# Block products summed in PSUM from a copy of the first one, and the pooled groups taken in the order 4, 16, 8, 2

## The chip, the cores and the metric

The kernel runs on one core of a Trainium2 chip. A core has engines that work beside each other, each through its own instructions in order: PE (matmuls into PSUM), DVE (elementwise work), ACT (activations, copies, casts), POOL (elementwise work, slower here) and SP, which issues DMA transfers. PSUM is the small memory that PE writes to and that DVE and ACT can read and write; SBUF is the large one. The metric is the device time of one execution in microseconds (us). The program is built by a scheduler that simulates the engines and puts each engine's instructions in an order of its own; priorities and "issue after" marks in the source steer it, and the order in the source is not the order on the chip.

## The reference

Two layers act on a stream of 1024 tokens by 1024 channels (and 256 context tokens, which only the first layer uses). The even layer adds a gated convolution branch and a gated recurrence branch. The odd layer, where most of this change lies, is a pooling mixer:

```
z = h @ w_in                       # 1024 -> 4096: u (2048), g (2048)
for group, w in enumerate((2, 4, 8, 16)):      # 512 channels of u each
    d[group] = mean of u over [t - w/2, t + w/2) in its row of 64 tokens - u
y = concat(d[group] @ w_grp[group]) * scale
x = x + gate * ((y * silu(g)) @ w_out)         # 2048 -> 1024
return rmsnorm(x, final_g)
```

`h` is the normalised stream, scaled and shifted by a conditioning vector. Everything is in float32.

## The kernel before, in words

**Numbers.** A float32 product is made of three products of a faster matmul type: a source is split in a high part (a cast on ACT, L94) and a low part (source minus high part, on DVE or POOL, L95), and high x high, high x low and low x high are accumulated in PSUM (`prod`, L595: 12 matmuls of 128 x 512 for a block of 512 input channels).

**Blocks.** Large projections go through `quad` (L610). It computes two tiles of 128 output channels over all 1024 tokens as a 2 x 2 block product in seven products instead of eight (Strassen's scheme in Winograd's form). The output block (i, h) is channel tile m + i, token half h. On the side of the activations the operands are sums of blocks (`block_sums`, L557: t1 to t4 beside b11, b21, b22, listed in `BOPS`, L51); on the side of the weights `wquad` (L567) loads two tiles of 128 x 1024, makes three sums and a difference on DVE (L583, L584, L585, L590) and splits all seven operands: 1 and 6 on DVE, 2, 5, 7, 4 and 3 on POOL. Then

- product 1 goes into the PSUM tile a, ACT copies it to SBUF as s1 (L616); product 6 goes into b, DVE writes s2 = b + s1 (L621); product 2 is accumulated on a, which is block (0,0);
- product 5 goes into c, ACT copies it to s3 (L629); product 7 is accumulated on b, DVE writes s1 = b + s1 (L636); block (1,1) is s3 + s1, added on POOL, since both are in SBUF;
- product 4 goes into a fourth tile d; block (1,0) is s1 - d, on DVE; product 3 is accumulated on c, and block (0,1) is s2 + c, on DVE.

`put` is what the caller does with a block. PSUM has four banks for such tiles (`psum`, L86). Evacuations have a raised priority (`EVAC`).

**Order of the work.** Up to 763 us: conditioning, norm, the even layer's projections and recurrence, and its gates. 763 to 848: the out-projection of its convolution branch, `woa` (L830), four quads, with each result added to a partial residual in memory (`added`, L802: load, gated add, store). 848 to 905: the norm, and folding of `w_in` with `w_grp`. 905 to 1254: the pooling mixer's input, eight pairs of quads (the loop at L1002, m = 0, 2, ..., 14): a quad of u, whose blocks go to padded tiles (`to_tokens`, L1011), then pooling on DVE (`pool`, L913: log2(w) shifted adds at L928, corrections at the row ends at L937 and L941, the difference at L946, for each of four tiles), and a quad of g with SiLU (`to_gate`, L1018). The product of the two (L1057) and its block sums go to memory (`y_keep`, `y_sums`). In the second to fifth pair two conditioning tiles for the second layer's gate are also computed on DVE (L205). 1254 to 1438: the out-projection in two halves of its input: part 0 in four quads (L1071, blocks added to the residual), part 1 in two quads (L1101) and two halves of a quad without products 5 and 3 (`last_half0`, L1182), whose remaining products come at the end in column pieces, between the steps of the final norm. 1438 to 1462: the last of the norm and the stores.

## Time and profile before

| what | value |
|---|---|
| median of three runs | 1466.99 us (1466.47 to 1467.98) |
| the profiled execution's own time | 1463.63 us |
| its span | 1461.8 us |
| mean granted clock of PE | 0.961 |
| PE busy | 1323.3 us (91%) |
| DVE busy | 1265.6 us (87%) |
| ACT busy | 639.2 us (44%) |
| POOL busy | 739.9 us (51%) |

A busy PE isn't PE at its best pace: matmuls overlap, and at a low granted clock each takes longer. So a stretch is best compared with the number of its matmuls times the distance of two of them at full pace. The idle time printed with a group of instructions is that of its engine just ahead of them, and the name behind it is what ended it. The prediction below shows the rows that it uses.

### The profile page before, as it was taken

How to read it: one execution, taken by the hardware profiler on the slowest of the kernel's cores; microseconds unless marked ns; L12 is line 12 of the kernel's file. 1: busy time of each engine (PE TensorE's matmuls, PEld its weight loads, DVE VectorE, ACT ScalarE, POOL GpSimd, SP SyncE). 2: the span in 40 equal slices, each digit the busy share in tenths (PEclk: the TensorE clock that was granted, in tenths of full speed). 3: DMA queues.
4: the chain of work that ended last, by engine and by line, in shares of the span. 5: the costliest groups of instructions: out<-in, count | busy, mean ns of one | idle time of the engine just before them, and what ended most of it. 6: DMA issues, size and time to landing. Idle time of an engine off the chain costs nothing. (4 is left out here: it accounts for less than half of the span.)

```text
span 1461.8 us, 15892 instructions
## 1 busy us (share of the span) xinstructions
PE 1323.3 (91%) x5664; PEld 1060.8 (73%) x5664; DVE 1265.6 (87%) x1445; ACT 639.2 (44%) x906; POOL 739.9 (51%) x398
## 2 busy tenths in 40 slices
PE   7799989897999889999998989999998997798896
PEld 4478767776777677888886877778777775577675
DVE  7985889798879899997878859999999999986985
ACT  6443584466457624226334345433332223433542
POOL 5273654664557456425327446555435536445642
PEclk9999999999999999999999999999999999899998
DMA  9741212121211223443542475133342135457723
GB/s 362 251 116 39 63 37 73 65 65 34 75 51 52 71 94 119 133 146 120 190 137 98 158 219 169 56 129 129 116 137 86 66 116 173 151 187 241 244 91 115
DMA packets 82867, 181.80 MB, mean 124 GB/s; under 512 B 7778, under 2 KB 27618, under 8 KB 82788
## 3 DMA queue, kind: packets, MB, share of 16 engines
q1 hardware_dynamic: 74340, 176.60, 36.7%
q10 hardware_dynamic: 8448, 4.20, 1.0%
q8 instruction: 44, 0.72, 0.2%
q14 instruction: 35, 0.29, 0.1%
HBM read 136.72 MB, written 44.04 MB: 124 GB/s over the span
## 5 line engine op out<-in xcount | busy, mean ns | idle before, releaser
L681 DVE SCALAR_TENSOR_TENSOR conv<-u,sm,conv 128x1009 f32<-128x1009 f32 (+14 forms) x240 | 300.8, 1272 | 21.9 <-ACT conv L674 18.7
L95 POOL TENSOR_TENSOR wl_wu<-wr_wu,wh_wu 128x1024 fp32r<-128x1024 f32 x16 | 38.7, 2422 | 68.4 <-ACT wh_wu L94 68.4
L95 POOL TENSOR_TENSOR wq_wo<-wr_wo,wq_wo 128x512 fp32r<-128x512 f32 x32 | 49.7, 1558 | 43.8 <-ACT wq_wo L94 42.5
L95 POOL TENSOR_TENSOR wq_g<-wr_g,wq_g 128x512 fp32r<-128x512 f32 x32 | 55.0, 1735 | 31.6 <-ACT wq_g L94 31.6
L94 ACT CAST wq_v<-wr_v 128x512 fp32r<-128x512 f32 x48 | 28.2, 619 | 91.3 <-DVE wr_v L585 45.5
L520 PE MATMUL g<-uh,wh_gw 128*128 128x512 f32 (+1 forms) x96 | 40.1, 419 | 25.7 <-ACT g L523 16.3
L95 POOL TENSOR_TENSOR wq_v<-wr_v,wq_v 128x512 fp32r<-128x512 f32 x32 | 55.3, 1744 | 14.8 <-ACT wq_v L94 11.1
L94 ACT CAST wq_g<-wr_g 128x512 fp32r<-128x512 f32 x48 | 28.2, 619 | 78.7 <-DVE wr_g L585 28.4
L523 ACT ACTIVATE g<-g,sm 128x512 f32<-128x512 f32 (+1 forms) x96 | 53.4, 623 | 18.0 <-PE g L522 10.1
L242 PE MATMUL fold<-gh,wh_wu 128*128 128x512 f32 x128 | 53.6, 420 | 6.3 <-ACT wh_wu L94 6.3
L439 POOL TENSOR_TENSOR g<-g,uc 128x1280 f32<-128x1280 f32 x16 | 47.4, 2963 | 19.9 <-ACT g L523 19.9
L124 PE MATMUL gb<-h0h,wh_gb 128*128 128x512 f32 x128 | 51.7, 404 | 5.5 <-ACT sb L662 5.5
L243 PE MATMUL fold<-gl,wh_wu 128*128 128x512 f32 x128 | 52.8, 413 | 3.7 <-DVE gl L95 3.7
L444 POOL TENSOR_TENSOR g<-g,g 128x1280 f32<-128x1280 f32 x16 | 50.6, 3176 | 9.6 <-ACT g L443 9.6
L457 POOL TENSOR_TENSOR g<-g,g 128x1024 f32<-128x1024 f32 x8 | 19.1, 2387 | 70.6 <-DVE g L454 70.6
L445 DVE SCALAR_TENSOR_TENSOR g<-a,g 128x1280 f32<-128x1280 f32 x16 | 37.1, 2316 | 20.3 <-POOL g L444 20.3
L244 PE MATMUL fold<-gh,wl_wu 128*128 128x512 f32 x128 | 51.7, 413 | 2.7 <-POOL wl_wu L95 2.7
L126 PE MATMUL va<-h0h,wl_va 128*128 128x512 f32 x128 | 49.6, 391 | 3.1 <-POOL wl_va L95 3.1
L125 PE MATMUL gb<-h0l,wh_gb 128*128 128x512 f32 x128 | 51.4, 401 | 0.0
L126 PE MATMUL gb<-h0h,wl_gb 128*128 128x512 f32 x128 | 50.9, 399 | 0.0
L125 PE MATMUL wob<-ybl,wh_wob 128*128 128x512 f32 x128 | 50.3, 394 | 0.0
L126 PE MATMUL ga<-h0h,wl_ga 128*128 128x512 f32 x128 | 50.2, 392 | 0.0
(577 smaller groups left out, 4802.4 us busy)
## 6 DMA issues: line engine op xcount, KB each, us to landing
mod<-modT SPq DMA_DIRECT2D x28, 512.0 KB, 3.9
wr_wu<-wu SPq DMA_DIRECT2D x16, 512.0 KB, 4.1
x_part<-xp SPq DMA_DIRECT2D x32, 256.0 KB, 3.2
xp<-x_part SPq DMA_DIRECT2D x32, 256.0 KB, 4.1
mod<-modT SPq DMA_DIRECT2D x32, 256.0 KB, 3.5
wr_v<-wfold SPq DMA_DIRECT2D x16, 512.0 KB, 3.5
wr_g<-wg SPq DMA_DIRECT2D x16, 512.0 KB, 4.4
yr_t<-y_t SPq DMA_DIRECT2D x16, 512.0 KB, 5.8
```

The lines of the kernel that those rows point to most:

```text
L94: return (nc.scalar.copy(hi, src), eng.tensor_tensor(out=lo, in0=src, in1=hi.bitcast(F32), op=sub))
L95: eng.tensor_tensor(out=lo, in0=src, in1=hi.bitcast(F32), op=sub))
L124: nc.tensor.matmul(ps, hi[:, kc], xh[k][:, cols], start=(k == 0), stop=False)
L125: nc.tensor.matmul(ps, hi[:, kc], xl[k][:, cols], start=False, stop=False)
L126: nc.tensor.matmul(ps, lo[:, kc], xh[k][:, cols], start=False, stop=(k == ks - 1))
L242: nc.tensor.matmul(ps, wh[:, kc], gh[i], start=(i == 0), stop=False)
L243: nc.tensor.matmul(ps, wh[:, kc], gl[i], start=False, stop=False)
L244: nc.tensor.matmul(ps, wl[:, kc], gh[i], start=False, stop=(i == 3))
L439: nc.gpsimd.tensor_tensor(out=ius[d], in0=ius[d], in1=uc, op=mult)
L444: nc.gpsimd.tensor_tensor(out=iu, in0=iu, in1=r, op=mult)
L523: nc.scalar.activation(t[:, a : a + n], ps[:, :n], AF.Sigmoid, bias=col(ob + d * KT + j))
L681: nc.vector.scalar_tensor_tensor(out=acp[:, a:b], in0=us[j][:, a + o : b + o], scalar=col(O_CONVW + 31 * j + k), in1=acp[:, a:b], op0=mult ...
```

## The change

**Products.** `quad` now uses three PSUM tiles. ACT copies product 1 from a into b, inside PSUM. Product 5 goes into c; its part for block (1,1) is handed on at once. Product 6 is accumulated on b, on top of the copy, and the part for block (0,1) is handed on; product 2 on a gives block (0,0). Product 7 on b completes block (1,1) with the kept part, product 3 on c completes block (0,1), and product 4 on b is block (1,0), which needs no add (the sign of t4 is turned for that). A part is kept by an ACT copy to SBUF (`keep_part`) or, where the block is added to a residual that lies in SBUF, added there by the gated DVE add, so that the second part is a second gated add. No add is left on POOL; `quad`'s additions on DVE (L621, L636) are gone. `last_half0` follows the same scheme, with product 4 in a tile of its own, second in order.

**Pooling order.** The host permutes the four groups of channels, in `w_in`, `w_grp`, `scale` and `w_out`, so that the loop meets the widths 4, 16, 8, 2 instead of 2, 4, 8, 16 (two pairs of quads each).

**Order of operands and loads.** `BOPS` and the splitting of the operands follow the new order of products. `wquad` splits operand 5 first on POOL, and 4 last; with `late` (the last weights) 4 before and 5 later. `woa` loads the partial residual straight into the tiles that it is added in. The weights of the next quad of part 0 wait for the last store of y, and the later operands of part 0 for the last SiLU.

```diff
-WINDOWS = (2, 4, 8, 16)
+GROUPS = (1, 3, 2, 0)
+WINDOWS = tuple(2 << g for g in GROUPS)
...
-BOPS = ("b11", "t2", "b21", "t1", "t3", "t4", "b22")
+BOPS = ("b11", "t1", "t2", "b21", "t3", "b22", "t4")
...
         p1 = op(a11, 1, nc.vector)
+        if late:
+            p4 = op(a22, 4, nc.gpsimd)
         s3 = ttile(f"ws_{name}")
         nc.vector.tensor_tensor(out=s3, in0=a11, in1=a21, op=sub)
         nc.vector.tensor_tensor(out=a21, in0=a21, in1=a22, op=add)
         nc.vector.tensor_tensor(out=a11, in0=a21, in1=a11, op=sub)
+        if not late:
+            p5 = op(a21, 5, nc.gpsimd)
         p6 = op(a11, 6, nc.vector)
         p2 = op(a12, 2, nc.gpsimd)
-        p5 = op(a21, 5, nc.gpsimd)
         p7 = op(s3, 7, nc.gpsimd)
         nc.vector.tensor_tensor(out=a12, in0=a12, in1=a11, op=sub)
-        p4 = op(a22, 4, nc.gpsimd)
+        if late:
+            p5 = op(a21, 5, nc.gpsimd)
         p3 = op(a12, 3, nc.gpsimd)
+        if not late:
+            p4 = op(a22, 4, nc.gpsimd)
...
-        a = psum(f"qa_{name}")
+        a, c, b = psum(f"qa_{name}"), psum(f"qc_{name}"), psum(f"qb_{name}")
         prod(a, p1, ops["b11"], True, False)
-        s1 = ttile(f"s1_{name}")
         with tc.high_priority(offset=EVAC):
-            evac_a = nc.scalar.copy(s1, a)
-        b = psum(f"qb_{name}")
-        prod(b, p6, ops["t2"], True, False)
-        s2 = ttile(f"s2_{name}")
+            evac = nc.scalar.copy(b, a)
+        prod(c, p5, ops["t1"], True, False)
         with tc.high_priority(offset=EVAC):
-            evac_v = nc.vector.tensor_tensor(out=s2, in0=b, in1=s1, op=add)
+            put(1, 1, c, 0)
+        prod(b, p6, ops["t2"], False, False)
+        with tc.high_priority(offset=EVAC):
+            put(0, 1, b, 0)
         prod(a, p2, ops["b21"], False, True)
         with tc.high_priority(offset=EVAC):
-            put(0, 0, a, None, None)
-        c = psum(f"qc_{name}")
-        prod(c, p5, ops["t1"], True, False)
-        s3 = ttile(f"s3_{name}")
-        with tc.high_priority(offset=EVAC):
-            nc.scalar.copy(s3, c)
+            put(0, 0, a, None)
...
-        prod(b, p7, ops["t3"], False, True)
+        prod(b, p7, ops["t3"], False, False)
         with tc.high_priority(offset=EVAC):
-            nc.vector.tensor_tensor(out=s1, in0=b, in1=s1, op=add)
-        with tc.high_priority(offset=EVAC):
-            put(1, 1, s3, s1, add)
-        d = psum(f"qd_{name}")
-        prod(d, p4, ops["t4"], True, True)
-        with tc.high_priority(offset=EVAC):
-            put(1, 0, s1, d, sub)
+            put(1, 1, b, 1)
         prod(c, p3, ops["b22"], False, True)
         with tc.high_priority(offset=EVAC):
-            put(0, 1, s2, c, add)
+            put(0, 1, c, 1)
+        prod(b, p4, ops["t4"], False, True)
+        with tc.high_priority(offset=EVAC):
+            put(1, 0, b, None)
         return w
+
+    def keep_part(parts, name, i, x):
+        parts[i] = ttile(f"s{i}_{name}")
+        nc.scalar.copy(parts[i], x)
...
     def woa(m, w, ahead):
-        def put(i, h, x, y, op):
-            if (i, h) == (0, 0):
-                for q in range(2):
-                    x1[m + q] = xtile(f"x1_{m + q}")
-            v = x1[m + i][:, HALF[h]]
-            added(m0, m, i, h, x, y, op, v)
-            square_acc(nacc[h][:, :H], v, (m, i) == (0, h), f"n1q{m}_{i}_{h}")
+        for q in range(2):
+            x1[m + q] = xtile(f"x1_{m + q}")
+
+        def put(i, h, x, part):
+            v, dr = x1[m + i][:, HALF[h]], x1_part[m + i][:, HALF[h]]
+            if part != 1:
+                nc.sync.dma_start(v, dr)
+            nc.vector.scalar_tensor_tensor(out=v, in0=x, scalar=m0[:, 0, 2 * KT + m + i : 2 * KT + m + i + 1],
+                                           in1=v, op0=mult, op1=add)
+            if part != 0:
+                nc.sync.dma_start(dr, v)
+                square_acc(nacc[h][:, :H], v, (m, i) == (0, h), f"n1q{m}_{i}_{h}")
         return quad(w, f"woa{m}", ya, put, ahead)
...
+        def to_tokens(i, h, x, part):
+            if part is None:
                 nc.scalar.copy(token[i][h], rows(x))
+            elif part == 0:
+                keep_part(parts, f"v{m}", i, x)
             else:
-                eng = nc.gpsimd if (i, h) == (1, 1) else nc.vector
-                eng.tensor_tensor(out=token[i][h], in0=rows(x), in1=rows(y), op=op)
-
-        def to_gate(i, h, x, y, op):
+                nc.vector.tensor_tensor(out=token[i][h], in0=rows(x), in1=rows(parts[i]), op=add)
+
+        def to_gate(i, h, x, part):
             v = ys[m + i][:, HALF[h]]
-            if y is None:
-                nc.scalar.activation(v, x, AF.Silu)
-            else:
-                eng = nc.gpsimd if (i, h) == (1, 1) else nc.vector
-                eng.tensor_tensor(out=v, in0=x, in1=y, op=op)
-                nc.scalar.activation(v, v, AF.Silu)
+            if part == 0:
+                keep_part(parts, f"g{m}", i, x)
+                return
+            if part == 1:
+                nc.vector.tensor_tensor(out=v, in0=x, in1=parts[i], op=add)
+                x = v
+            silu[0] = nc.scalar.activation(v, x, AF.Silu)
...
+    def gated(k, v, x):
+        return nc.vector.scalar_tensor_tensor(out=v, in0=x, scalar=m1[:, 0, 2 * KT + k : 2 * KT + k + 1],
+                                              in1=v, op0=mult, op1=add)
+
     for m in range(0, KT, 2):
-        def put(i, h, x, y, op):
-            added(m1, m, i, h, x, y, op)
+        parts = {}
+
+        def put(i, h, x, part):
+            if part == 0:
+                keep_part(parts, f"wo0_{m}", i, x)
+                return
+            t = vtile(f"xp{m}_{i}_{h}")
+            nc.sync.dma_start(t, x1_part[m + i][:, HALF[h]])
+            if part == 1:
+
+                s = x if i == 0 else parts[i]
+                nc.vector.tensor_tensor(out=s, in0=x, in1=parts[i], op=add)
+                x = s
+            gated(m + i, t, x)
+            nc.sync.dma_start(x1_part[m + i][:, HALF[h]], t)
...
     def last_half0(m, w, ahead=None):
         p1, p2, p3, p4, p5, p6, p7 = w
-        a = psum(f"qa_l{m}")
+        a, d, b = psum(f"qa_l{m}"), psum(f"qd_l{m}"), psum(f"qb_l{m}")
+        (x0, x1_), (y0, y1) = [[x1[m + i][:, h] for h in HALF] for i in range(2)]
         prod(a, p1, ops["b11"], True, False)
...
+            evac = nc.scalar.copy(b, a)
+        mm = prod(d, p4, ops["t4"], True, True)
         with tc.high_priority(offset=EVAC):
-            evac_v = nc.vector.tensor_tensor(out=s2, in0=b, in1=s1, op=add)
+            gated(m + 1, y0, d)
...
+            prod(b, p6, ops["t2"], False, False)
         with tc.high_priority(offset=EVAC):
-            gated(m, x1[m][:, HALF[0]], a)
+            gated(m, x1_, b)
+        mm = prod(a, p2, ops["b21"], False, True)
+        with tc.high_priority(offset=EVAC):
+            gated(m, x0, a)
             fin_add(HALF[0], square(m, HALF[0]))
-        mm = prod(b, p7, ops["t3"], False, True)
+        with tc.issue_after(mm.ins):
+            mm = prod(b, p7, ops["t3"], False, True)
         with tc.high_priority(offset=EVAC):
...
+            gated(m + 1, y0, b)
             fin_add(HALF[0], square(m + 1, HALF[0]))
-            vec = gated(m + 1, x1[m + 1][:, HALF[1]], s1)
+            vec = gated(m + 1, y1, b)
```

84 lines of the change are left out of this document (30 added, 54 removed).

## The prediction, made before the changed kernel had run

> **What bounds the kernel now.** I read, in this order, the table of busy time by stretch, the waits of PE, the groups of DVE and POOL, and the timeline at single stalls. First the stretches (length; then busy time and instruction count of PE, weight loads, DVE, ACT, POOL; then granted clock, DMA share, GB/s), those that the change reaches; the third to fifth row are the pairs of quads in which the pooling mixer's input is computed: first pair, six middle pairs, last pair; then the out-projections.
>
> ```profile
> 675.30:763.20 87.90, 87.90 (x387) 72.43 (x386) 69.35 (x143) 36.56 (x50) 28.60 (x14) 1.00 0.47 153
> 763.20:848.00 84.80, 78.11 (x326) 61.21 (x324) 69.98 (x70) 35.49 (x61) 49.26 (x31) 0.98 0.41 130
> ...
> 905.40:1254.30 348.90, 317.64 (x1345) 256.03 (x1344) 326.73 (x418) 117.91 (x207) 172.27 (x111) 0.98 0.35 114
> ```
> ```profile
> 905.58:953.00 47.42, 41.89 (x169) 33.02 (x168) 44.58 (x52) 25.77 (x44) 26.65 (x26) 0.93 0.26 84
> 953.00:1202.58 249.58, 234.74 (x1009) 190.76 (x1008) 232.62 (x314) 73.28 (x133) 117.70 (x71) 0.99 0.34 110
> 1202.58:1254.57 51.99, 41.10 (x170) 32.31 (x168) 49.62 (x54) 18.96 (x30) 27.73 (x15) 0.97 0.49 159
> 1254.57:1437.90 183.33, 161.66 (x664) 128.91 (x662) 149.57 (x151) 75.53 (x117) 97.43 (x56) 0.93 0.51 174
> ```
>
> The pace of PE alone comes from the first matmuls of two products that follow each other (start, duration):
>
> ```profile
> 971.89 0.39 PE L599 MATMUL qc_v<-x_b22h,wq_v 128*128 128x512 f32 x1
> ...
> 974.62 0.39 PE L599 MATMUL qa_g<-x_b11h,wq_g 128*128 128x512 f32 x1
> ```
>
> Twelve matmuls take 2.73 us, 0.2275 each; a quad (84) is 19.1, a pair 38.2. The eight pairs would take 305.8 at this pace and take 348.9: 43.1 over. The out-projections after them hold 672 matmuls' worth (six quads, two last halves of 60, 24 of 512 columns and 48 of 256), 152.9, and take 183.3: 30.4 over. Before 905 only the first out-projection (336 matmuls, 76.4; 84.8 taken) is touched; the stretch ahead of it is full of PE. So the change plays for about 80 us at most. In the middle pairs DVE is busy 232.62 of 249.58, 38.8 a pair, more than PE's own 38.2. This is what PE waits for there, and what it waits for in the out-projections (in all, times, longest):
>
> ```profile
> PE qa_v L599 <- ACT s_v L616: 9.7, 4, 3.0
> PE qb_g L599 <- DVE s_g L621: 6.3, 4, 3.7
> PE qb_v L599 <- DVE s_v L621: 3.8, 2, 2.4
> PE qb_v L601 <- DVE x_t2l L877: 3.3, 2, 2.6
> PE qc_g L599 <- DVE vp L1016: 2.1, 1, 2.1
> PE qb_v L602 <- DVE wq_v L95: 2.0, 1, 2.0
> ```
> ```profile
> PE qb_wo L599 <- DVE s_wo L621: 5.2, 2, 3.9
> PE qb_wo L599 <- ACT wq_wo L94: 4.7, 1, 4.7
> PE qa_wo L599 <- DVE s_wo L636: 3.7, 1, 3.7
> PE qa_wo L599 <- ACT s_wo L616: 3.0, 2, 1.9
> PE qa_l L599 <- ACT s_l L1188: 2.6, 1, 2.6
> PE qb_wo L602 <- DVE wq_wo L95: 1.2, 1, 1.2
> ```
>
> Nearly all are waits for the evacuation of a product that stands late in DVE's order, or in ACT's behind something of DVE's. The bound is DVE's backlog, seen through PSUM.
>
> **The change, part by part.** The groups of the eight pairs (busy, mean ns | idle before):
>
> ```profile
> L928 DVE TENSOR_TENSOR ws<-ws 128x616 f32<-128x616 f32 (+2 forms) x45 | 46.1, 1025 | 0.8
> ...
> L590 DVE TENSOR_TENSOR wr_g<-wr_g 128x512 f32<-128x512 f32 x8 | 14.1, 1768 | 2.3 <-POOL wq_g L95 2.3
> L205 DVE SCALAR_TENSOR_TENSOR mod<-mod,cL 128x1024 f32<-128x1024 f32 x8 | 13.5, 1688 | 0.0
> ...
> L585 DVE TENSOR_TENSOR wr_g<-wr_g,wr_g 128x512 f32<-128x512 f32 x8 | 5.5, 685 | 0.0
> L621 DVE TENSOR_TENSOR s_v<-qb_v,s_v 128x512 f32<-128x512 f32 x8 | 5.5, 684 | 0.0
> ...
> L636 DVE TENSOR_TENSOR s_v<-qb_v,s_v 128x512 f32<-128x512 f32 x8 | 5.4, 681 | 0.0
> L1016 DVE TENSOR_TENSOR vp<-s_v,qd_v 128x512 f32<-128x512 f32 x8 | 5.4, 676 | 0.0
> ```
> ```profile
> L95 POOL TENSOR_TENSOR wq_g<-wr_g,wq_g 128x512 fp32r<-128x512 f32 x32 | 55.0, 1735 | 31.6 <-ACT wq_g L94 31.6
> ...
> L1016 POOL TENSOR_TENSOR vp<-s_v,s_v 128x512 f32<-128x512 f32 x8 | 13.3, 1659 | 39.3 <-ACT wq_g L94 35.5 <-DVE s_v L636 3.8
> L1024 POOL TENSOR_TENSOR y<-s_g,s_g 128x512 f32<-128x512 f32 x7 | 11.3, 1619 | 65.4 <-ACT wq_v L94 40.8 <-PE qc_g L602 12.9 <-DVE s_g L636 11.7
> ```
>
> *DVE and POOL in the pairs.* Each quad loses L621 and L636 on DVE; of the combining adds two stay there (for blocks (1,1) and (0,1)), as now two (for (1,0) and (0,1)). That is 4 x 0.68 = 2.7 us a pair. POOL loses its add, 1.66 and 1.62 a pair. A DVE instruction that reads SBUF alone takes 0.69 undisturbed (L585) and 1.77 where it lies beside POOL's splits (L590), so each POOL add gone returns up to 1.1 of DVE time: 0 to 2.2 a pair. DVE's 38.8 falls to 33.9 to 36.1, under PE's 38.2, where the pooling is of mean width. I take 3.8 less, between the two: DVE's instructions of this size on SBUF are found at 0.69 as well as at 1.77, and no row says which of them a POOL add meets.
>
> *The pooling order.* A width w takes log2(w) adds (L928) in each of a pair's four tiles. Width 16 has 16 a pair against 10 in the mean, 6.2 us more at 1.025; width 2 has 6.2 less. The modulation (L205) lies in the second to fifth pair, 3.4 each against 2.2 in the mean of the middle six. So by DVE's work: the third and fourth pair (now width 16, with modulation) 38.8 + 6.2 + 1.2 - 3.8 = 42.4, of which I let 1 pass into the light neighbours: 41.5 each. Second (width 4, -2.1) 34 and sixth (width 8, without modulation, +2.1 - 2.2) 35 go by PE with 1.1 left over: 39.3 each. Fifth (width 8, with it) 38.3: 39.5. Seventh and eighth (width 2) 27: 38.5 and 39, in place of 41.6 (the mean of the middle six) and 52.0. The first stays at 47.4: it has the operands' splits (the wait for L877 among them), and its own pooling grows by four adds, 4.1, which is what the edit returns. The sum is 47.4 + 39.3 + 2 x 41.5 + 39.5 + 39.3 + 38.5 + 39 = 326.0 against 348.9: **-23**. Bounds: middle pairs all at PE's pace and the last too, -20.3 - 13.8 = -34; or, if the new waits below take back half, -11.
>
> *What the new chain makes wait.* Products 1, 6, 7, 4 now go through one bank. The copy of product 1 on ACT goes from PSUM to PSUM. The nearest row of that kind is the gate's activation in place (count, shortest/median/longest ns), against the copies to SBUF:
>
> ```profile
> L771 ACT ACTIVATE ga<-ga x16: 576/580/582, 682.0 to 763.6; 128x512 f32<-128x512 f32 x16
> ```
> ```profile
> L616 ACT COPY s_v<-qa_v 128x512 f32<-128x512 f32 x8 | 4.6, 570 | 0.0
> ```
>
> So its price is the same. In the changed program's order on PE, 24 matmuls of other products stand between product 1 and product 6 (5.5 us for the copy), 56 between 6 and 7 (12.7 for ACT's keeping of the partial sum), 23 between 7 and 4 (5.2 for DVE's add of (1,1)), and 17 between 4 and the next user of its bank (3.9 for ACT). ACT gets three instructions more a pair, 1.8 at 0.59, beside 73.28 busy in 249.58: nothing, while ACT's order lets them through. The copy stands behind a weight cast that waits for the DMA and a DVE sum, the add of (1,1) behind the sum for the third weight, which waits for a POOL split (2.3 idle in eight, L590). Both covers are larger than one such wait; DVE's lateness, which eats them today, shrinks. Cost 0, taken back in rival B.
>
> *Weights.* Per quad the loop is: load (a row of the chain of waits: start, duration), DVE sums, casts, five POOL splits (5 x 1.74 = 8.7), among them DVE's last sum. Today POOL's add can stand ahead of the splits (timeline):
>
> ```profile
> 1084.03 4.39 DMA wr_g<-wg
> ```
>
> ```profile
> 1052.88 1.79 POOL L1016 TENSOR_TENSOR vp<-s_v,s_v 128x512 f32<-128x512 f32 x1 [11.81 <-ACT wq_g L94]
> 1054.64 2.98 POOL L95 TENSOR_TENSOR wq_g<-wr_g,wq_g 128x512 fp32r<-128x512 f32 x2
> ```
>
> Its 1.7 goes; product 5's split, moved ahead of 2 and 7, is then in time for its place as second product. No separate gain.
>
> *The out-projections of the pooling mixer.* L621 and L636 go (5.2 and 3.7 of the waits), of which I count two thirds, 6, for the next in line is the shared bank's own chain. The 4.7 and 1.2 for weights come from DVE, which is still pooling with width 16 when they start (on DVE, and PE's stall):
>
> ```profile
> 1270.68 1.33 DVE L941 TENSOR_TENSOR ws<-ws,eg 128x56 f32<-128x56 f32 x1
> ...
> 1272.05 2.80 DVE L946 SCALAR_TENSOR_TENSOR vp<-ws,vp 128x512 f32<-128x512 f32 x1
> ```
> ```profile
> 1262.60 0.80 PE L599 MATMUL qb_wo<-y_t2h,wq_wo 128*128 128x512 f32 x1 [4.65 <-ACT wq_wo L94]
> ```
>
> With width 2 there most of it goes: 5. **-11**; bounds 0 and -18 (all waits of the fence but 3).
>
> *The first out-projection.* The blocks' residual is now loaded straight into its tile, three DVE instructions fewer a quad; but the loads stand in SP's queue before the next weights, and the first quad's raw weights come free later, after up to two POOL splits more (3.3). Three of its four quads are nearly at PE's pace already, and its 8.4 over lies mostly at the start: **+1**, between -3 and +4.
>
> *The end.* In the last halves product 4 fills the time of the copy (2.6, L1188), two DVE instructions fewer each: **-1**, 0 to -2.6. Moved x operands, SP's fewer issues: 0 within +-1, hidden by the first pair's splits.
>
> **Sum.** -23 - 11 + 1 - 1 = -34 against the profiled execution of 1463.63, which gives 1430. The median of the runs is 1466.99, 3.4 above it: **1433**.
>
> **The clock.** The 43.1 over are 31.3 of idle PE and 11.8 of slow matmuls (317.64 busy against 305.8). A stall of 3.04 is followed by matmuls of 0.71, not 0.39:
>
> ```profile
> 1043.41 0.71 PE L599 MATMUL qa_v<-x_b21h,wq_v 128*128 128x512 f32 x1 [3.04 <-ACT s_v L616]
> ```
>
> My pairs' lengths take this in, since they are measured whole. The Trainium skill, "TensorE: Matmul & The Clock Gate", section "What's actually happening", says the clock halves after an idle window of about 3.4 us. By that only one wait of the pairs (3.7) would pay, an estimate of 1.7, the gain there would be about 5 less, and the forecast 1438; the row at 1043 shows shorter stalls paying.
>
> **Rivals.** *A, the gain is eaten:* ACT takes its queue in order, and both products 6 and 2 now hang on the copy. The 9.7 us for L616 speak for it: that wait isn't removed but doubled. Against it: its cause is DVE's lateness. If such waits stay at the present size and the heavy pooling beside modulation gives 43 in two pairs, 2 to 15 remains: about 1457.
>
> *B, slower:* the chain on one bank. If DVE's add of (1,1) lands later than the 5.2 us, product 4 stalls in each of 28 quads and halves; at 34 / 28 = 1.2 us a time the gain is gone, and at 2 us it is 28 x 2 - 34 = 22 more: 1489. For it: DVE waits up to 3.7 today show DVE that late (L621). Against: DVE has more room. The skill's same page, section "A second HAM failure mode: psum-queue depth-cycling", says that passing through PSUM banks makes PE pause and its clock swing; the row from 675.30, four banks passing every 24 matmuls, has 1.00 and no idle. No row here shows three.
>
> *C, no change:* weights set the pace. From load to DVE's last sum it is some 20 us of the loop now (4.4 load, sums, casts, 8.7 of splits, 1.7 of the add); if the loop stays at 20.8 a quad, the time stays 1467. Against it: no row of PE's waits in the pairs names weights for more than 2.0.
>
> **How the numbers follow.** Forecast 0.68, A 0.12, B 0.16, C 0.04. The forecast's own range is 1414 to 1452, from the bounds of the pairs (-34, -11) and projections. The range 1412 to 1462 holds the forecast and most of A. A measurement here can tell 0.2% (3 us) from no change; faster is forecast and A, 0.80, same C, 0.04, slower B, 0.16.
>
> **What would show it.** Right: L621 and L636 absent, DVE under 36 us a light pair, pairs of 38 to 42 with the third and fourth the longest, the last under 41, wo0's first weights not waited for. Wrong: PE waits on qb for ACT's copy or for DVE's add of (1,1) in most quads (A or B), a granted clock under 0.95 in the pairs (B), or waits for wq (C).

## The result

The changed kernel takes 1459.95 us (median of 7 runs, 1455.93 to 1463.59) against 1467.35 for the one before (7 runs): a ratio of 0.9948, 95% interval 0.9937 to 0.9960. It is faster by 7.4 us, where 34 were forecast.

The profiled execution of the changed kernel took 1463.59, the slowest of its seven, and the one before 1463.63, faster than any of its seven. So the two profiles show where time moved, and not the 7.4 us themselves. The part ahead of the first out-projection is nearly the same program in all kernels here, and yet the pairs begin between 901 and 909 us; lengths of stages are therefore compared. Executions of one kernel lie 2 to 15 us apart, and each length comes from a single one: a difference of a few us between two profiles is a hint, and the larger claims lean on the medians beside them.

The stretches of the changed kernel (columns as in the prediction): the first out-projection, the norm and folds, the first pair, the six middle pairs, the last pair, the second out-projections, the end.

```profile
765.10:851.00 85.90, 76.99 (x316) 61.05 (x315) 63.91 (x67) 37.15 (x63) 47.78 (x30) 0.94 0.44 147
851.00:908.43 57.43, 52.81 (x235) 42.40 (x234) 40.14 (x47) 26.68 (x43) 27.63 (x12) 1.00 0.56 170
908.43:951.18 42.75, 34.62 (x133) 26.59 (x132) 40.34 (x46) 25.15 (x43) 23.53 (x21) 0.92 0.25 80
951.18:1206.37 255.19, 235.82 (x1009) 190.19 (x1008) 231.81 (x312) 86.60 (x157) 99.31 (x60) 0.99 0.33 110
1206.37:1262.30 55.93, 48.10 (x194) 38.85 (x192) 43.18 (x45) 23.40 (x37) 27.13 (x15) 0.91 0.57 169
1262.30:1436.60 174.30, 156.57 (x669) 127.18 (x667) 124.06 (x125) 75.19 (x115) 82.13 (x47) 0.96 0.52 178
```

The eight pairs take 42.75 + 255.19 + 55.93 = 353.9, not 326 as forecast and 349.0 before. The out-projections took 183.1 before, measured to the same point, and take 174.3.

The matmul counts of these rows matter for what follows. Before, each pair, from its first product to that of the next, holds 168 matmuls. In all kernels with the new products PE's order lets products slip past that mark: the first pair holds 132, one later pair 192 (the last one here, the fifth with the old pooling order; a row counts one or two more at its edges), and all eight 1332 instead of 1344, since the last product of the last quad comes after the first one of the out-projections. At 0.2275 us each, 36 matmuls are 8.2 us, 24 are 5.5 and 12 are 2.7. So the first pair's 42.75 and the last one's 55.93 can't be read beside 47.4 and 52.0 as they stand. Above PE's own pace the pairs are 353.9 - 1332 x 0.2275 = 50.8, before 43.2: they lost 7.6 at equal work. The out-projections, counted in the same way, are 24.8 above PE's pace and were 35.7.

DVE's busy time in the pairs fell from 326.8 to 315.3 and POOL's from 172.1 to 150.0, but PE is idle for 35.3 us in them, and was for 31.3 before, only for other things:

```profile
PE qb_g L607 <- ACT qb_g L625: 9.6, 3, 4.2
PE qb_v L607 <- DVE vp L1022: 7.0, 2, 3.9
PE qb_g L610 <- DVE wq_g L96: 4.7, 2, 3.0
PE qb_g L607 <- ACT wq_g L95: 4.2, 2, 3.6
PE qc_g L607 <- ACT s_g L653: 3.6, 1, 3.6
```

L625 is the copy inside PSUM, L1022 the add of (1,1), L653 a kept part, L95 and L96 the weights' split. One of these stalls, followed back through the timelines of PE, ACT, DVE and SP, shows how it comes about:

```profile
1237.95 0.50 PE L607 MATMUL qb_g<-x_t2h,wq_g 128*128 128x512 f32 x1 [4.21 <-ACT qb_g L625]
```
```profile
1231.16 0.62 ACT L95 CAST wq_g<-wr_g 128x512 fp32r<-128x512 f32 x1 [4.96 <-DVE wr_g L588]
1235.75 1.14 ACT L95 CAST wq_g<-wr_g 128x512 fp32r<-128x512 f32 x2 [3.97 <-DVE wr_g L589]
1236.80 0.61 ACT L95 CAST wq_g<-ws_g 128x512 fp32r<-128x512 f32 x1
1237.32 0.58 ACT L625 COPY qb_g<-qa_g 128x512 f32<-128x512 f32 x1
```
```profile
1229.83 0.69 DVE L562 TENSOR_TENSOR y<-y,y 128x512 f32<-128x512 f32 x1 [4.29 <-DMA y_b<-y]
1230.44 0.69 DVE L588 TENSOR_TENSOR wr_g<-wr_g 128x512 f32<-128x512 f32 x1
1231.04 3.01 DVE L928 TENSOR_TENSOR ws<-vp 128x632 f32<-128x632 f32 x1
1233.97 1.75 DVE L589 TENSOR_TENSOR wr_g<-wr_g,wr_g 128x512 f32<-128x512 f32 x1
```
```profile
1226.12 0.32 SPq L1088 DMA_DIRECT2D xp<-x_part  x1
1226.53 0.38 SPq L956 DMA_DIRECT2D y_b<-y  x1
```

Read it from the bottom. A store of the gated product leaves SP at 1226.53, behind a load of the residual that waited 4.3 us for its tile. DVE must overwrite the stored tile with the fourth block sum (L562) and stands still for 4.29 us until the store has read it. Behind L562 in DVE's order are the weights' sums (L588, L589), with a pooling add of 3.01 us (L928) between them. ACT's casts wait for those, and behind the casts in ACT's order is the copy a to b, which PE waits for. In the kernel before the same sum (L561 there) had 0.1 us of idle time ahead of it in all the pairs:

```profile
L561 DVE TENSOR_TENSOR y<-y,y 128x512 f32<-128x512 f32 x7 | 4.8, 687 | 0.1
```

Block (1,0) was not the last one there, and the last one, (0,1), isn't stored by itself.

### The profile page after: what moved, and what is told of

Read it like the earlier page. It is cut to its first block, busy times and chain, and to the rows that moved or that the text cites. A ratio compares the mean times of both kernels' runs of the same rounds, so it can differ in the third digit from the quotient of the medians.

```text
span 1461.8 us, 15776 instructions
## 1 busy us (share of the span) xinstructions
PE 1320.6 (90%) x5664; PEld 1060.1 (73%) x5664; DVE 1220.5 (83%) x1389; ACT 653.0 (45%) x928; POOL 695.8 (48%) x372
## 5 line engine op out<-in xcount | busy, mean ns | idle before, releaser
L688 DVE SCALAR_TENSOR_TENSOR conv<-u,sm,conv 128x1009 f32<-128x1009 f32 (+14 forms) x240 | 301.0, 1273 | 21.7 <-ACT conv L681 18.5
L96 POOL TENSOR_TENSOR wq_v<-wr_v,wq_v 128x512 fp32r<-128x512 f32 x32 | 54.3, 1712 | 84.6 <-ACT wq_v L95 84.4
L96 POOL TENSOR_TENSOR wq_g<-wr_g,wq_g 128x512 fp32r<-128x512 f32 x32 | 49.8, 1567 | 91.8 <-ACT wq_g L95 91.5
L96 POOL TENSOR_TENSOR wq_wo<-wr_wo,wq_wo 128x512 fp32r<-128x512 f32 x32 | 49.1, 1542 | 58.4 <-ACT wq_wo L95 48.6
L96 POOL TENSOR_TENSOR wl_wu<-wr_wu,wh_wu 128x1024 fp32r<-128x1024 f32 x16 | 39.4, 2467 | 73.6 <-ACT wh_wu L95 73.6
L95 ACT CAST wq_g<-wr_g 128x512 fp32r<-128x512 f32 x48 | 28.2, 619 | 94.7 <-DVE wr_g L588 33.9
L95 ACT CAST wq_v<-wr_v 128x512 fp32r<-128x512 f32 x48 | 28.2, 619 | 81.0 <-DVE wr_v L595 29.3
L521 PE MATMUL g<-uh,wh_gw 128*128 128x512 f32 (+1 forms) x96 | 40.7, 425 | 25.8 <-ACT g L524 16.3
L440 POOL TENSOR_TENSOR g<-g,uc 128x1280 f32<-128x1280 f32 x16 | 47.4, 2961 | 19.6 <-ACT g L524 19.6
L95 ACT CAST wq_wo<-wr_wo 128x512 fp32r<-128x512 f32 x48 | 28.8, 619 | 58.9 <-DVE wr_wo L588 15.0
L928 DVE TENSOR_TENSOR ws<-ws 128x616 f32<-128x616 f32 (+2 forms) x48 | 52.3, 1091 | 0.9
L127 PE MATMUL gb<-h0h,wl_gb 128*128 128x512 f32 x128 | 50.8, 398 | 0.0
```

What stands on the lines that cost most here:

```text
L95: return (nc.scalar.copy(hi, src), eng.tensor_tensor(out=lo, in0=src, in1=hi.bitcast(F32), op=sub))
L96: eng.tensor_tensor(out=lo, in0=src, in1=hi.bitcast(F32), op=sub))
L127: nc.tensor.matmul(ps, lo[:, kc], xh[k][:, cols], start=False, stop=(k == ks - 1))
L688: nc.vector.scalar_tensor_tensor(out=acp[:, a:b], in0=us[j][:, a + o : b + o], scalar=col(O_CONVW + 31 * j + k), in1=acp[:, a:b], op0=mult ...
L928: nc.vector.tensor_tensor(out=nxt[:, :, a_:b_], in0=cur[:, :, a_ + o0 : b_ + o0], in1=cur[:, :, a_ + o1 : b_ + o1], op=add)
```

## The experiments

All lengths below are of one profile per kernel: "pairs" is from the first product of the first pair to that of the second out-projections, "projections" from there to the first column sums of the final norm (183.1 before, 174.3 after). Medians and ratios are against runs of the kernel before on the same chip.

### The pooling order and the rest of the change, apart

The first kernel undoes the order in the changed kernel, the second puts it alone into the kernel before.

```diff
-GROUPS = (1, 3, 2, 0)
+GROUPS = (0, 1, 2, 3)
```

> The changed kernel with the pooling widths back in the order 2, 4, 8, 16; everything else stays. Theory A (the width 16 beside the modulation costs the third to fifth pair what the light end should have returned): third and fourth pair fall from 45.5 and 43.6 to about 40, the last one stays near 52, the time is 1452 or less. Theory B (each pair's length is set by the loop of the weights: load, DVE's place for the sums, POOL's splits): the pairs' lengths move only with how late DVE's sums are, the total within 4 us of 1460. Theory C (the one bank for products 1, 6, 7, 4 is the new bound): the same waits of products 4 and 6 in any order, 1460.

> The kernel before, its seven products and adds unchanged, with the pooling widths in the order 4, 16, 8, 2. Theory A: the third and fourth pair grow by 4 to 6 each, the last pair falls from 52 to 42: 1467 to 1470. Theory B: the last pair stays above 50, since it waits for the reloaded operands of the out-projection, and the out-projections gain up to 10: 1460 to 1467. If the order alone brings the 7 us, the new products bring nothing.

The old order in the changed kernel: 1463.59, ratio 0.9974 (0.9957 to 0.9991); pairs 349.5, projections 182.5. The new order in the kernel before: 1474.55, ratio 1.0051 (1.0032 to 1.0071); pairs 361.9, projections 180.9. So the order lengthens the pairs, by 12.9 in the kernel before and by 4.4 in the changed one, the former after 6 returned by the last pair (52.0 to 45.9), while in the changed kernel the last pair grows with it (47.3 to 55.9; 5.5 of that are the 24 matmuls that it holds with the new order). In the changed kernel it returns 8.2 in the projections. The third and fourth pair of the old order are 39.4 and 41.8, as theory A had it, but the fifth is 53.2, with 192 matmuls 9.5 above PE's pace; A's 1452 did not come.

The row of the eight pairs with the old order tests the prediction's theory directly:

```profile
904.67:1254.20 349.53, 314.94 (x1334) 253.47 (x1333) 301.02 (x390) 133.04 (x232) 140.49 (x95) 0.97 0.36 115
```

DVE is busy for 25.8 us less than before (301.0 against 326.8), near the forecast's 30, and the pairs are no shorter (349.5 against 349.0). PE still waits for DVE there, 21.2 us for the add of (1,1), but for a DVE that stands still (15.9 us for the store), not for one with too much work. With the new order DVE's gain looks like 11.5 only because the pairs then hold more of the pooling: that order alone puts 14 DVE instructions more into the pairs of the kernel before (432 against 418) and 11 fewer into the projections (140 against 151).

### The weights first on DVE

```diff
-        wq = wquad([wg[m + i] for i in range(2)], f"g{m}", ring_x)
+        with tc.high_priority(offset=EVAC):
+            wq = wquad([wg[m + i] for i in range(2)], f"g{m}", ring_x)
```

(The same for `v_weights`.)

> The changed kernel with the weights' sums, casts and splits of the eight pairs raised to the priority of the evacuations, so that they stand ahead of the pooling in DVE's order. Theory B: PE's waits for split weights and for copies that stand behind casts (9.6 + 4.7 + 4.2 + 1.5 us in the pairs) go, the middle pairs fall to 39 to 41, the time to about 1445. Theory A and C: no gain, or a loss where the evacuations now stand behind the sums: 1458 to 1470.

1462.42, ratio 0.9966 (0.9944 to 0.9987), pairs 354.8: no gain. DVE's order came out almost the same as in the changed kernel, so this did not test theory B.

### The fourth block sum in a tile of its own

```diff
-        eng.tensor_tensor(out=b21, in0=b21, in1=b11, op=sub)
+        eng.tensor_tensor(out=t4, in0=b21, in1=b11, op=sub)
```

(`t4` is a tile of the pool "t".)

> The changed kernel with the fourth block sum of the gated product written to a tile of its own, so that DVE needn't wait until the store of block (1,0) has read the tile (5.9 us of DVE's waits in the middle six pairs and 4.3 in the last one). If that wait, which holds up the weights' sums behind it, sets the pairs' pace: pairs three to five shorter by 1 to 2 each, the last by 4, 1450 to 1455. If DVE only moves its lateness elsewhere: 1458 to 1462.

1454.44, ratio 0.9914 (0.9894 to 0.9933); pairs 342.1, 11.8 less than in the changed kernel. DVE's waits for the store are gone from the middle pairs. What they were in the changed kernel, and what is left (DVE's waits, middle pairs):

```profile
DVE mod L206 <- DMA mod<-modT: 6.3, 4, 2.0
DVE y L562 <- DMA y_b<-y: 5.9, 4, 2.1
```
```profile
DVE mod L206 <- DMA mod<-modT: 8.2, 4, 2.8
DVE wq_v L96 <- ACT wq_v L95: 3.6, 4, 1.4
```

In this pair of profiles the waits of 5.9 + 4.3 us cost about as much as they lasted; by the medians the tile brings 5.5 (1459.95 to 1454.44). It is the part of the change that took back most.

### The same with the old order

> The kernel with the fourth block sum in a tile of its own (1454), with the pooling widths in the order 2, 4, 8, 16. Open: whether the order 4, 16, 8, 2, which lost 7 us in the kernel before and stood 4 better in the changed kernel, costs the pairs anything. If the order costs the pairs 10 and returns it in the out-projections: the pairs' sum 332 to 336 against 342, the out-projections 8 longer, the time 1452 to 1456. If the order is good by itself: 1457 to 1462, with product 4 waiting for the add of (1,1) for 15 us or more.

1453.82, ratio 0.9898 (0.9863 to 0.9933); pairs 337.5, projections 184.8. Against `t4_own` (342.1 and 179.2) the order again costs the pairs 4.6 and returns 5.6 in the projections; by the medians it makes no difference here. The tile of its own takes 12.0 off the pairs in this order too (349.5 to 337.5); the waits for the store that went with it were 15.9 us, six of them, up to 5.4. Here five of the six middle pairs are within 2.1 us of PE's pace with all splits on POOL; what is left lies in the first, the fifth and the last pair.

### Three more waits taken away, each on top of the tile of its own

Pooling behind the add of (1,1):

```diff
-                pool(m + i, h, vps[2 * i + h])
+                with tc.issue_after(parts[1, 1].ins):
+                    pool(m + i, h, vps[2 * i + h])
```

> The kernel with the fourth block sum in a tile of its own (1454), and in each pair the pooling of all four tiles put behind DVE's add of block (1,1) in DVE's order. Theory C (product 4 stands behind that add, which DVE reaches only after the pooling of the first tile; 7.0 us of PE's waits in the changed kernel, 21.2 with the old pooling order): PE no longer waits for it, the pairs three to five shorten by 1 to 2 each, 1447 to 1451. Theory D (DVE's order only passes the lateness on; something else will wait): the wait goes and the time stays within 3 us of 1454, or grows since the pooling of the last tile and the gated product come later.

The modulation in the fifth to eighth pair:

```diff
-        elif m <= KT:
-            n = 2 * KT + m - 2
+        elif m >= KT:
+            n = KT + m
```

> The kernel with the fourth block sum in a tile of its own, and the modulation (two tiles of 512 KB loaded and two DVE sums a pair) moved from the second to fifth pair to the fifth to eighth. Theory A (width 16 beside the modulation): third and fourth pair fall by 3 to 5 each, the later ones rise by 0 to 2 since they have width 8 and 2: 1446 to 1452. If the modulation's work isn't what makes those pairs long: same lengths, 1452 to 1457. The last pair can lose, if its operand loads queue behind the modulation's.

The first residual loads behind the stores:

```diff
+            with ExitStack() as sctx:
+                if m == 0:
+                    sctx.enter_context(tc.issue_after(stored[0].ins))
+                nc.sync.dma_start(t, x1_part[m + i][:, HALF[h]])
```

> The kernel with the fourth block sum in a tile of its own, and the four loads of the residual for the first out-projection quad put behind the last store of the gated product in SP's queue. If one of these loads, waiting for its tile, holds the stores and reloads behind it (4.3 us of SP's waits in the last pair): the last pair falls from 49.8 by 2 to 4, 1450 to 1453. If not: 1453 to 1456, or a loss of 1 to 3 in the first out-projection quad, whose residual comes later.

| kernel | median | ratio (95%) | pairs | projections |
|---|---|---|---|---|
| `add_first` | 1452.29 | 0.9887 (0.9864 to 0.9910) | 337.6 | 182.9 |
| `mods_late` | 1448.72 | 0.9869 (0.9840 to 0.9898) | 342.1 | 178.9 |
| `xp_late` | 1449.92 | 0.9875 (0.9850 to 0.9899) | 341.4 | 177.4 |

The intervals overlap with that of `t4_own`, two of them barely, so none is clearly shown to gain by itself. `add_first` does what it says to PE's wait for the add of (1,1), but PE then waits 10.2 us in six places for the low part of a weight (product 6): theory D's picture. With `mods_late` the second to fourth pair are 38.7, 38.1 and 39.4, so width 16 alone doesn't bind; the pairs that took the modulation over lost as much.

### Fewer splits on POOL

Two of POOL's five splits of a weights' block are left out; PE does as many matmuls with the high part.

```diff
+            if i in (3, 4) and name[0] in "vg":
+                nc.scalar.copy(t[:, HALF[0]], v)
+                high_only.append(t)
+                return t
...
+        low = 0 if any(t is w for t in high_only) else H
```

> The kernel with the fourth block sum in a tile of its own, leaving out the low parts of the weights' operands 3 and 4 in the eight pairs (PE takes the high part again in their place, as many matmuls; the output isn't the reference's): POOL has 3 splits a quad instead of 5, 6.8 us less a pair. Theory B (the loop of the weights through POOL's splits and two raw tiles sets the pace) and theory E (POOL's splits slow DVE, whose instructions on SBUF lose 60 us in the middle six pairs beside them): the middle pairs fall to about 39 each and DVE's busy time by 2 to 4 a pair, 1440 to 1446. If neither: 1452 to 1456.

> The kernel before, leaving out the low parts of the weights' operands 3 and 4 in the eight pairs (PE takes the high part again; the output isn't the reference's). Leaving them out took 14 us off the changed kernel's pairs (the one with the fourth block sum in its own tile). Theory B/E (POOL's splits already set the pairs' pace before the change, not DVE's adds): about as much here, the pairs' sum 333 to 338, the time 1453 to 1458. The prediction's theory (DVE's own work, 38.8 a pair, sets the pace): only what DVE gets back, under 5: 1462 to 1467.

> The kernel with the fourth block sum in a tile of its own and without the low parts of operands 3 and 4 in the eight pairs (the output isn't the reference's), with the order 2, 4, 8, 16: the same light POOL and the same order as in the kernel before without those splits, whose middle pairs run at PE's pace (38.1 each, sum 324.0). What is left of a difference is the new chain of products alone. If the one bank costs nothing: 324 and 38.1 a pair. If it costs what its waits show in the other runs: 328 to 336, with waits of product 4 for the add of (1,1).

On the changed kernel with its own tile: 1440.49, pairs 327.7. On the kernel before: 1440.99, ratio 0.9810 (0.9793 to 0.9827), pairs 324.0. On the changed kernel with its own tile and the old order: 1439.61, pairs 324.5. The six middle pairs of the kernel before without these splits:

```profile
956.80:1186.20 229.40, 228.86 (x1010) 189.21 (x1009) 210.77 (x314) 74.36 (x133) 71.05 (x47) 1.00 0.36 121
```

They run at PE's own pace, 38.2 a pair, PE is busy 228.86 of 229.40, and all of DVE's adds of the old scheme are in them. DVE is busy 210.77, where the same 314 instructions took 232.62 beside the full number of splits. So a tenth of DVE's busy time was POOL's doing, and DVE's work, 35.1 a pair here, is under PE's pace. This run alone doesn't tell whether the pairs were long because POOL stretched DVE (theory E) or because POOL's splits held up the weights (theory B); two of the runs below separate these. The Trainium skill, "SBUF — State Buffer", section "Who interferes with whom", says that a DVE instruction with two SBUF inputs contends with a POOL instruction that reads SBUF; these 22 us agree. The new chain of products costs little once POOL is light. The eight pairs of the changed kernel with the old order, and of the kernel before, both without the splits:

```profile
900.94:1225.40 324.46, 309.08 (x1334) 252.29 (x1333) 277.77 (x389) 133.64 (x232) 92.88 (x62) 0.98 0.36 123
909.40:1233.40 324.00, 313.22 (x1346) 255.42 (x1345) 298.46 (x421) 120.23 (x207) 114.23 (x80) 0.98 0.37 123
```

The lengths agree, but the first holds 12 matmuls less, so at equal work it is 3.2 longer (21.4 above PE's pace against 18.2), and the agreement is a sum of unlike parts: its last pair is 3.6 above PE's pace against 9.0, its fifth is 6.0 above it, where the other kernel's is at it. PE waits 5.7 us for the add of (1,1) in it.

### POOL's add moved to DVE in the kernel before

```diff
-                eng = nc.gpsimd if (i, h) == (1, 1) else nc.vector
-                eng.tensor_tensor(out=token[i][h], in0=rows(x), in1=rows(y), op=op)
+                nc.vector.tensor_tensor(out=token[i][h], in0=rows(x), in1=rows(y), op=op)
```

(The same in `to_gate`.)

> The kernel before, with the add of block (1,1) on DVE instead of POOL in the eight pairs: POOL loses 3.3 us a pair, DVE gains two adds of SBUF operands, 1.4 a pair undisturbed. The prediction took up to 2.2 a pair of DVE time back from each pair's POOL adds. If that holds: DVE's busy time in the middle six pairs stays or falls, 1460 to 1467. If a POOL instruction gone gives DVE nothing, as the changed kernel's 60.6 us of DVE lengthening beside 60.2 before suggest: DVE grows by 1.4 to 2.2 a pair and the time by 3 to 12, 1470 to 1480.

1460.71, ratio 0.9946 (0.9928 to 0.9963): as much as the whole change, if by other stages (the projections, which gained in the changed kernel, don't here: 184.9). The eight pairs:

```profile
903.41:1248.60 345.19, 318.96 (x1345) 256.69 (x1344) 330.17 (x432) 120.73 (x210) 150.40 (x96) 0.97 0.35 114
```

Here DVE has 16 adds more (14 in the rows) and is busy 330.2 us, 3.4 more than before, and the pairs are 3.8 shorter. More work on DVE, less on POOL, and it is faster. The 16 adds are 11 us at 0.69, so each POOL add gone returned an estimated 0.5 us to DVE, 1.0 a pair, inside the prediction's 0 to 2.2.

### The raw weights freed earlier

POOL's splits of operands 3 and 4 read a standing tile in place of the raw weights.

```diff
+            if i in (3, 4) and name[0] in "vg":
+                hi = t[:, HALF[0]]
+                nc.scalar.copy(hi, v)
+                eng.tensor_tensor(out=t[:, HALF[1]], in0=bx["b11"][0][0].bitcast(F32), in1=hi.bitcast(F32), op=sub)
+                return t
```

> The kernel with the fourth block sum in a tile of its own (1454), where POOL's splits of operands 3 and 4 in the eight pairs read a standing tile instead of the raw weights (wrong low parts, so the output isn't the reference's): POOL is as busy and disturbs DVE as much, but the raw tiles come free for the next load some 3 us a quad earlier. Theory B (the loop of the weights through two raw tiles): most of the 14 us that the left-out splits brought, 1440 to 1446. Theory E (POOL's splits slow DVE): 1452 to 1456.

1446.70 (1441.74 to 1452.34), ratio 0.9852 (0.9822 to 0.9882), pairs 330.9. The eight pairs with the tile of its own, with the raw weights freed earlier, and with the splits left out:

```profile
907.76:1249.90 342.14, 316.20 (x1334) 253.50 (x1332) 311.89 (x398) 135.28 (x234) 146.29 (x96) 0.97 0.36 117
901.87:1232.80 330.93, 311.70 (x1333) 251.30 (x1332) 306.49 (x396) 132.81 (x231) 143.47 (x94) 0.98 0.36 121
902.44:1230.10 327.66, 311.23 (x1333) 252.82 (x1332) 284.50 (x398) 133.32 (x231) 97.51 (x62) 0.98 0.36 123
```

POOL's work is the same, DVE is stretched nearly as much (306.5 against 311.9), and still the pairs lose 11.2 of the 14.4 that the left-out splits brought. Leaving them out frees 22 us of DVE in addition and brings only 3.3 more. By the medians it is 7.7 of 14.0, since the second profile is the fastest execution of its kernel. So at least half of POOL's effect is the loop of the weights: the two raw tiles are free for the next load only when POOL has split them. This is shown for the kernel with the new products; the same edit in the kernel before wasn't run. SP's queue shows the loads held in both kernels (middle pairs; before, then after):

```profile
SPq L571 <- POOL wq_g L95: 64.1, 12, 9.6
```
```profile
SPq L573 <- POOL wq_g L96: 59.6, 12, 10.3
SPq L573 <- POOL wq_v L96: 54.9, 12, 9.2
```

Such waits alone don't show a cost: with the splits left out SP waits nearly as long for ACT's casts (56.6 and 45.7), while four of the six middle pairs run within 1.5 us of PE's pace.

### A gap among the splits, which was not the cause

```diff
+        if not late:
+            p4 = op(a22, 4, nc.gpsimd)
         p3 = op(a12, 3, nc.gpsimd)
-        if not late:
-            p4 = op(a22, 4, nc.gpsimd)
```

> The changed kernel with POOL's split of operand 4 put back ahead of that of operand 3. In the changed kernel POOL stands idle inside nearly every batch of five splits, 1.3 to 3.0 us each time and 33 us over the twelve quads of the middle six pairs, until DVE's last sum and ACT's cast for operand 3 are done; in the kernel before the split of 4 stood there and no such gap shows. If the weights' loop sets the pace and this gap is what the add taken off POOL gave back: the pairs' sum falls by 10 to 25 from 353.9, the time to 1440 to 1452. If other waits (the store of block (1,0), the copy behind casts) hold the loop anyway: 1455 to 1462.

> The same with the fourth block sum in a tile of its own, so that DVE's sums for the weights don't wait for the store either (342.1 in the pairs, 1454, without this edit). If both hold up the same loop one after the other: the pairs' sum 322 to 334, the time 1436 to 1447. If the split's gap doesn't matter: 1452 to 1457.

With this alone 1468.11, ratio 0.9985 (0.9968 to 1.0001), pairs 353.3, projections 181.0; with the tile of its own 1455.78, ratio 0.9907 (0.9880 to 0.9933), pairs 340.6. The theory falls: the pairs don't shorten at all. PE waits 19.5 us for DVE's add of (1,1) in the first of them instead of 7.0, and the projections lose most of what the change had brought (181.0 against 174.3). With the tile of its own the split's place makes no difference there (179.2 with and without).

### The edits together

> The changed kernel with the four edits together: the fourth block sum in a tile of its own, the pooling behind the add of (1,1), the modulation in the fifth to eighth pair, the first residual loads behind the last store. If the gains add up (5.5, 2.2, 5.7, 4.5): 1442. If they are one lateness taken away at several places: 1446 to 1450, not better than the best one alone.

> The changed kernel with the four edits together (1439), and in the last quad of the pairs the two kept parts copied by DVE instead of ACT. Open: why the last pair is 50 to 56 us in spite of width 2. If it is ACT's order (the copy of c stands behind casts of the out-projection's operands, which wait for their reload): product 3's wait of 6.3 us goes and the last pair falls from 56 to 48 to 51, the time to 1432 to 1436. If the reload itself is late, PE waits as long at the first out-projection quad: 1437 to 1441.

> The kernel with the four edits together (1439, pairs 341.4, projections 165.7) and POOL's split of operand 4 ahead of 3. If the gap is what still holds its pairs: sum 325 to 334, time 1424 to 1433. If the pairs are held by the last pair's reloads and DVE's order: 1436 to 1441.

The four edits together: 1438.96 (1435.41 to 1439.97), ratio 0.9794 (0.9776 to 0.9812), the fastest of all with the full computation. But its pairs are 341.4, no shorter than with the tile alone; the gain is in the projections, 165.7:

```profile
1247.30:1413.00 165.70, 155.56 (x669) 125.28 (x667) 114.51 (x125) 75.29 (x116) 83.03 (x48) 0.98 0.56 192
```

There the scheduler gave PE another order, in which product 4 comes later and never waits for the add of (1,1), which in the changed kernel costs 11.3 us in three places (PE's waits there, in the changed kernel):

```profile
PE qb_wo L607 <- DVE s_wo L1092: 11.3, 3, 6.2
PE qb_wo L607 <- DVE x L1077: 4.5, 1, 4.5
```

The second is product 7's wait for a gated add of the same kind. With either of two further edits that gain is lost again, and the waits for the add are back (10.1 and 11.2 us): the kept parts of the last quad on DVE give 1447.29, ratio 0.9858 (0.9826 to 0.9890), projections 176.7; operand 4's split ahead gives 1451.19, ratio 0.9874 (0.9853 to 0.9896), projections 179.4. So this version rests on an order that small edits upset. The last pair stays at 54 to 56 in all three. With the kept part on DVE product 3 still waits 5.1 us for it, so ACT's order alone is not what holds it. Of its length 5.5 are the 24 matmuls that it holds more; why it is still 10.6 to 12.5 above PE's pace in these three kernels stays open.

## Why the prediction was wrong

**The bound.** "The bound is DVE's backlog, seen through PSUM" is the step that failed. Three measurements speak against DVE's work as the bound. With the old pooling order the change took 25.8 us off DVE's busy time in the pairs, and they stayed at 349.5 against 349.0. In the kernel before, DVE with 3.4 us more and POOL with less made the pairs 3.8 shorter. And freeing the raw weights earlier, with DVE nearly as busy, took 11.2 off (7.7 by the medians). DVE's 38.8 a pair was taken for work; with fewer splits on POOL the same instructions take 35.1 (210.77 / 6), and the pairs run at PE's pace with every old add in place. The forecast's own sign, DVE under 36 in a light pair, came: 34.0 in the seventh pair (width 2), which still took 40.9.

What the runs show in its place is, for a large part, the loop of the weights through two raw tiles: load, DVE's sums, ACT's casts, POOL's splits. That was rival C's mechanism, at 0.04. For the kernel with the new products the run that frees the tiles earlier shows it; for the kernel before it is inferred from the light POOL and the moved add. And it is not all: the wait for the store was as large. Rival C's price was in the text ("its 1.7 goes", "no separate gain"): moving the one POOL add to DVE brings 6.7 us (1467.45 to 1460.71). That this equals the gain of the whole change is chance, since there the pairs grew and the projections gained. The argument against C, that PE's waits hardly name weights, doesn't hold, since a wait names only the last link: the stall at 1237.95 is named for the copy, which stood in order behind the casts and sums. In the kernel before no stall was followed back in this way.

**The pairs, -23, measured +4.9** (+7.6 at equal work). The measured figure leans on the changed kernel's slowest execution, but even if the whole 7.4 of the medians lay in the pairs they would be 2.5 shorter, far from the forecast's smaller bound, 11. With the old pooling order the profiles give a closed sum: 349.0 before; 345.2 with POOL's add on DVE; 337.5 with the new products but the fourth sum in its own tile; 349.5 as the change makes it; 353.9 with the new order. So: POOL's adds -3.8, the new products and the order of weights -7.7 (2.7 of it the product that moved behind the pairs' end), the wait for the store +12.0, the pooling order +4.4; the terms of about 4 are within what single profiles can differ by. The prediction had no term for the store: it doesn't ask what reads the block that is now last, after it is written. Of DVE's 3.8 a pair, 30 in all, 25.8 came with equal work in the pairs; the term was nearly right in size and bought nothing.

**The pooling order.** The third and fourth pair were forecast at 41.5 and measured 45.5 and 43.6. That the order would lengthen the pairs as a whole, by 12.9 in the kernel before, was not a term. The last pair was put at 39, since its 52.0 were laid to width 16. Measured are 55.9 at width 2, 50.5 without the 24 matmuls that it holds more.

**The new chain, 0.** Nearly right (3.2 at equal work with a light POOL), partly by luck, since in that run a longer fifth pair is balanced by a shorter last one. Its waits are there: 9.6 for the copy and 7.0 for the add in the pairs, in the place of 9.7 for the old copy and 10.1 for the old sums (L621). Rival B's stalls occur (up to 6.7 us with the old order) in a few quads, not in all 28.

**The out-projections, -11, measured -8.8** (183.1 to 174.3; -10.9 above PE's pace). Right in size, and luck has a part in it: the weights' waits of 5.9 are gone, but product 4's wait for the add, 11.3, stands in the place of the 8.9 of L621 and L636; and the gain comes only with the new order (182.5 without) and is 179.2 in the kernel with the fourth sum in its own tile.

**The first out-projection, +1:** 84.8 to 85.9. A quad there has two DVE instructions fewer (six in place of eight), not three as the prediction counts. **The end, -1:** from the final norm's first sums to the end 25.2 against 24.1, no gain that one profile can show.

Rival A's number, 1457, came nearest. Its mechanism, the copy held in ACT's order and heavy pooling beside the modulation, is in the trace, but only a part of the cause. The range 1412 to 1462 holds the measured 1459.95 because it takes in most of A; the forecast's own range, 1414 to 1452, doesn't. Its upper end doesn't follow from the bounds named for it either: -11 in the pairs and 0 in the projections give 1456.

## What to carry to other kernels

An engine that is busy for more than the pace of the bound may be stretched by its neighbour: before counting its instructions as work, compare them with the same form undisturbed, and follow the loop that feeds the buffers (load, transform, free) once round. Before comparing two stretches, count the matmuls in each: a reordered program moves work across the mark. When the order of results changes, look at what is done with the new last one: a store of it and an overwrite in place now stand at the end, and everything behind them in the queue waits too. A gain that rests on an order which a scheduler chose can vanish with the next edit, so it has to be measured by stage.

## What the runs showed of the hardware

The copy from PSUM to PSUM on ACT (L625) took 0.58 us, like a copy to SBUF, as expected. Not expected was how much a wait of DVE for a store matters: without four waits of at most 2.1 us and one of 4.3 (with the old pooling order six, 15.9 in all) the pairs were 12 us shorter.
